# A kernel of two hybrid layers: 128x128 tiles turned by VectorE in 32x32 blocks in place of TensorE

## The chip, the cores and the metric

One core of one Trainium2 chip runs the whole kernel. The metric is the device time of one execution in microseconds; the kernel before takes 1930.4 us (median of 3 runs, 1929.9 to 1931.18).

## What is computed

Two layers (`DEPTH = 2`) over 256 tokens of width 2048. Each layer normalises x, multiplies it by one wide input weight, and gives the slices to four branches of width 512 (4 heads x 128): A, attention over keys that an indexer selects; B, chunked retention with rotary phase; C, a gated linear recurrence (HGRN2); M, attention into 256 memory tokens. Each branch is gated, projected, weighted by a sigmoid gate and summed; an output projection is added to x.

```python
h = rms_norm(x, norm_g)
u = h @ w_in
...
y_a = sparse_index_attention(head_rms_norm(heads(a_q), qk_g[0]), head_rms_norm(heads(a_k), qk_g[1]), ...)
y_b = retention(rope(heads(b_q), cos, sin), rope(heads(b_k), cos, sin) * HEAD_DIM ** -0.5, heads(b_v))
y_c = head_rms_norm(hgrn2(f, heads(c_i), heads(c_q)), hgrn_g)
y_m = memory_attention(head_rms_norm(heads(m_q), qk_g[2]), head_rms_norm(heads(m_k), qk_g[3]), heads(m_v))
for n, (y, z) in enumerate(((y_a, a_z), (y_b, b_z), (y_c, c_z), (y_m, m_z))):
    branch = y.reshape(B, S, W).astype(dt) * jax.nn.silu(z)
    merged = merged + jax.nn.sigmoid(gate_all[:, :, n]) * (branch @ w_branch[n])
return x + merged @ w_out
```

## The kernel before

All large products run on TensorE (PE). Both factors are split into a rounded part and a remainder (`hi`, `lo`), and each product is three matmuls, hi x hi, hi x lo and lo x hi (lines 234 to 236). The weights stream in as blocks of 512 rows by 512 columns (1024 KB, a few of 328 or 256 columns); `split_weights` (L201 to L210) cuts each block into two halves of 256 rows: ScalarE (ACT) casts a half to `whi` (L208), VectorE (DVE) subtracts to get `wlo` (L209). There are 674 such pieces, nearly all of 128x1024. A half feeds 12 matmuls of 128x512: 2 slices of 128 rows x 2 blocks of 128 tokens x 3 products. The pool holds `HL = 4` buffers each of `whi` and `wlo`, so the two engines can be at most four halves ahead of PE: the cast of half h waits until half h-4 is multiplied out, and every `wlo` stands in the one queue of DVE with all other work of DVE.

PE is in the order: memory keys and values for both layers (`mk`, `mv`), then per layer 16 projections (`u`), 16 pairs of gate projection and branch projection (`u`, `bw`), and 4 output projections (`wo`). The small work of the branches is written as generators. After each half `gemms` calls `stream.pump()` (L239), which lets the first task in the list that can move take one step up to its next `yield`; where a product needs a task's result, `finish` runs the task to its end. The order inside DVE, ACT, PE and GpSimd (POOL) is then set by the framework's scheduler, so that instructions of different halves can change places; SP's order is as written.

Wherever an operand has to be turned from tokens-by-channels to channels-by-tokens, `transposed` (L270) issues eight 128x128 transposes on PE against the identity `ident` into a PSUM tile (L275); attention turns its probabilities the same way (L377), the indexer its keys and queries (L404, L412). ACT then copies the PSUM tile to SBUF, often together with a scale or a sigmoid (L251, L311, L379, L406, L414, L467, L500, L508). One 128x1024 tile is eight such blocks. POOL does some elementwise products and sums (L330, L339, L390, L401, L461, L714) and the powers of `rsq` (L268).

Two places are followed below. In `head_norm` (L327) of the HGRN2 branch, with names that begin with `cn`: square (`cnsq`, ACT), sum (`cnss`, DVE), `cnv` (DVE), power (`cnr`, POOL), two products (`cny`), turn, split (`cnh` on ACT, `cnl` on DVE). In `attend` (L346) for the memory branch: `mlg` (logits, PE), `mmx` (row maximum, DVE), `mnm`, four exponentials (`mp`, ACT), `mrc` (reciprocal, DVE), turn (`mpT`), product with the values (`mov`, PE).

Of the kernel before, what the change touches and what calls it, by code (L numbers as in the profile page):

```python
# [91 lines left out]
class Stream:  # L92
    def __init__(self):
        self.loaded = self.cut = self.used = 0
        self.raw, self.parts, self.tasks = deque(), deque(), []
# [5 lines left out]

    def pump(self):
        for t in list(self.tasks):
            moved = t.step()
            if t.done:
                self.tasks.remove(t)
            if moved:
                return True
        return False

    def finish(self, t):
        while not t.done:
# [3 lines left out]
            elif not moved:  # L116
                ahead = self.tasks[:self.tasks.index(t)]
                assert any(u.step() for u in ahead)
# [31 lines left out]
def trunk(ctx: ExitStack, tc: tile.TileContext, x, xt, memt, ng, qkg, hg, lbl, win, wmem, wbr, wout,  # L150
# [120 lines left out]
    def transposed(src, name):  # L271
# [4 lines left out]
        return ps  # L276

# [12 lines left out]
    def normed_t(ps, rs, g, name):  # L290
# [16 lines left out]
        def turn():  # L307
            yield
            pt = transposed(qn, name + "pt")
            qt = G([128, 4, 256], name + "t")  # L310
            ac.activation(qt, pt, AF.Copy, scale=g)  # L311
            return qt
# [11 lines left out]
    def branch_t(y, name):  # L324
        return split(transposed(y, name + "pt"), gen, "g", name)

    def head_norm(ps, zs, g, name):  # L327
        v = ps.rearrange("p (a d) -> p a d", a=8)
        zg = G([128, 2, 512], name + "zg")
        po.tensor_tensor(zg, zs, g[:, None, :].to_broadcast([128, 2, W]), op=OP.mult)  # L330
# [8 lines left out]
        po.tensor_tensor(y, y1.rearrange("p (t h) d -> p t (h d)", t=2), zg, op=OP.mult)  # L339
        yield  # L340
        yield
        return branch_t(y, name)

    def attend(box, names, keys, name):
# [6 lines left out]
        for t in range(2):  # L351
# [22 lines left out]
            pp = PB(f"{name}pp{t}")[:, :4 * nk].rearrange("p (h s) -> p h s", h=4)  # L374
            for h in range(4):
                for b in range(nb):
                    te.transpose(pp[:, h, b * 128:b * 128 + 128], p[:, h, b * 128:b * 128 + 128], ident)  # L377
            pt = G([128, 4, nk], f"{name}pT{t}")
            ac.copy(pt, pp)  # L379
# [10 lines left out]
            po.tensor_tensor(y[:, t, :], on.rearrange("p h d -> p (h d)"), zs[:, t, :], op=OP.mult)  # L390
            yield
        yield
        yield
        yield
        return branch_t(y, name)

    def selection(qi0, qi1, name):
# [3 lines left out]
        po.tensor_copy(kk, qi1[:, :, None, 256:320].to_broadcast([128, 2, 2, 64]))  # L401
        ps = PB(name + "kp")
        for t in range(2):
            te.transpose(ps[:, t * 128:t * 128 + 128], kk[:, t].rearrange("p a d -> p (a d)"), ident)  # L404
        kit = G([128, 256], name + "kt")
        ac.copy(kit, ps[:, :256])  # L406
        yield
        ps = PB(name + "qp").rearrange("p (b t) -> p b t", b=4)
        for b in range(4):
            src = (qi0, qi1)[b // 2]  # L410
            for t in range(2):
                te.transpose(ps[:, b, t * 128:t * 128 + 128], src[:, t, (b % 2) * 128:(b % 2) * 128 + 128], ident)  # L412
        qit = G([128, 4, 256], name + "qt")
        ac.copy(qit, ps)  # L414
# [33 lines left out]
    def rope_t(ps, rs, name):  # L448
# [12 lines left out]
        po.tensor_tensor(a, a, b, op=OP.add)  # L461

        def turn():
            yield
            pt = transposed(a, name + "pt")
            o = G([128, 4, 256], name + "t")
            ac.copy(o, pt)  # L467
            return o
# [28 lines left out]
    def hgrn_scores(uf, uq, lb, olb, name):  # L497
        pf = transposed(uf, name + "fp")
        f = G([128, 4, 256], name + "f")
        ac.activation(f, pf, AF.Sigmoid)  # L500
# [5 lines left out]
        pq = transposed(uq, name + "qp")  # L506
        q0 = G([128, 4, 256], name + "q0")
        ac.copy(q0, pq)  # L508
# [134 lines left out]
    for l in range(L):  # L643
# [51 lines left out]
        def merged(acc, d):  # L695
            yield
            return split(transposed(acc, "mgp"), gen, "g", f"mg{d}")

        mg = []
        for d in range(4):  # L700
            acc = G([128, 2, 512], f"acc{d}")
            for i, n in enumerate(BR_ORDER):
# [9 lines left out]
                else:  # L712
                    ve.tensor_mul(gt, pb, gt)  # L713
                    (ve if i == 3 else po).tensor_tensor(acc, acc, gt, op=OP.add)  # L714
            mg.append(stream.add(merged(acc, d)))

        def turned(c, xc, nssq, l=l):
            yield
            r = split_scaled(transposed(xc, "xp"), ngs[:, l + 1, 4 * c:4 * c + 4], xtp, "xt", f"x1{c}")
# [67 lines left out]
```

## Time and profile before

| | |
|---|---|
| median of 3 runs | 1930.4 us |
| span of the profiled execution | 1928.6 us |
| PE busy | 1917.2 us, 99% |
| DVE busy | 1077.5 us, 56%, 1130 instructions |
| ACT busy | 884.1 us, 46% |
| POOL busy | 131.9 us, 7% |
| granted TensorE clock | 1.000 |

The span runs from the first to the last instruction of the profiled execution. Busy time of an engine counts stretches in which at least one of its instructions runs. A row of the groups gives line, engine, operation, tiles and shapes, count, then busy time and mean length of one in ns, then how long the engine stood idle before and for whom. A row of the waits names who waited for whom, with total, number of times and the longest. A row of the timeline gives start, length, engine, line, tiles and count.

### The profile page before, as it was taken

What the parts mean: (1) busy time and instruction counts of PE and PEld (TensorE: products, weight loads), DVE (VectorE), ACT (ScalarE), POOL (GpSimd) and SP (SyncE); (2) the same over time, 40 slices, a digit from 0 to 9 for tenths busy, and PEclk for the clock granted to TensorE, in tenths of its full rate; (3) what the DMA queues carried; (4) which work ended last, traced back from release to release, by engine and by line L of the source; (5) the groups of instructions that cost most, each with busy time, mean ns of one, the idle gap of its engine ahead of it and who ended that gap; (6) DMA issues with size and microseconds to landing.
All of it is one profiled execution on the core that took longest, in us unless ns stands there. A gap on an engine that the chain in (4) does not pass through costs nothing.

```text
span 1928.6 us, 22255 instructions
## 1 busy us (share of the span) xinstructions
PE 1917.2 (99%) x9068; PEld 1605.0 (83%) x9068; DVE 1077.5 (56%) x1130; ACT 884.1 (46%) x1011; POOL 131.9 (7%) x63
## 2 busy tenths in 40 slices
PE   8999999999999999999999999999999999999999
PEld 7888988888888888888888898888888888888887
DVE  6646685556555455545554658555555555555454
ACT  6543445445544444444445344544554444444442
POOL 0200100101010000001000010020101000000100
PEclk9999999999999999999999999999999999999999
DMA  9653555454455555555555354544445555555553
GB/s 370 231 202 110 187 173 176 165 185 165 162 196 195 190 186 194 196 195 190 183 191 194 107 191 171 178 172 175 174 158 193 195 196 185 189 196 194 197 195 111
DMA packets 53606, 357.36 MB, mean 185 GB/s; under 512 B 6272, under 2 KB 6656, under 8 KB 12544
## 3 DMA queue, kind: packets, MB, share of 16 engines
q1 hardware_dynamic: 53504, 355.94, 52.2%
q8 instruction: 71, 1.16, 0.2%
q14 instruction: 31, 0.25, 0.0%
HBM read 353.82 MB, written 2.10 MB: 185 GB/s over the span
## 4 chain that ended last, share of the span: by engine, by line
PE 99%; DMA 0%; ACT 0%; SPq 0%; issue 0%; DVE 0%; DVEq 0%; ACTq 0%
PE u L234 24%; PE u L235 23%; PE u L236 23%; PE wo L236 3%; PE wo L235 3%; PE bw L236 3%; PE bw L235 3%; PE bw L234 3%; PE wo L234 3%; PE cl L525 1%; PE mv L235 1%; PE mv L236 1%; PE mv L234 1%; PE mk L235 1%; PE mk L234 1%; PE mk L236 1%
## 5 line engine op out<-in xcount | busy, mean ns | idle before, releaser
L209 DVE TENSOR_TENSOR wlo<-raw,whi 128x1024 fp32r<-128x1024 f32 (+2 forms) x674 | 831.6, 1236 | 743.6 <-ACT whi L208 742.7
L208 ACT CAST whi<-raw 128x1024 fp32r<-128x1024 f32 (+2 forms) x674 | 696.3, 1034 | 975.8 <-PE u L236 764.5
L714 POOL TENSOR_TENSOR acc<-acc,gate 128x1024 f32<-128x1024 f32 x16 | 51.6, 3226 | 736.9 <-DVE gate L713 712.9
L234 PE MATMUL u<-whi,x11h 128*128 128x512 f32 (+2 forms) x256 | 99.3, 388 | 0.0
L234 PE MATMUL u<-whi,x10h 128*128 128x512 f32 (+2 forms) x256 | 98.8, 386 | 0.5 <-ACT qi L284 0.5
L234 PE MATMUL u<-whi,x00h 128*128 128x512 f32 (+2 forms) x256 | 98.7, 386 | 0.5 <-ACT qi L284 0.5
L234 PE MATMUL u<-whi,x01h 128*128 128x512 f32 (+2 forms) x256 | 99.3, 388 | 0.0
L235 PE MATMUL u<-wlo,x12h 128*128 128x512 f32 (+2 forms) x256 | 98.7, 386 | 0.0
L235 PE MATMUL u<-wlo,x02h 128*128 128x512 f32 (+2 forms) x256 | 98.7, 386 | 0.0
L235 PE MATMUL u<-wlo,x03h 128*128 128x512 f32 (+2 forms) x256 | 98.6, 385 | 0.0
L235 PE MATMUL u<-wlo,x13h 128*128 128x512 f32 (+2 forms) x256 | 98.6, 385 | 0.0
L236 PE MATMUL u<-whi,x13l 128*128 128x512 f32 (+2 forms) x256 | 98.6, 385 | 0.0
L236 PE MATMUL u<-whi,x03l 128*128 128x512 f32 (+2 forms) x256 | 98.6, 385 | 0.0
L234 PE MATMUL u<-whi,x02h 128*128 128x512 f32 (+2 forms) x256 | 98.6, 385 | 0.0
L234 PE MATMUL u<-whi,x12h 128*128 128x512 f32 (+2 forms) x256 | 98.6, 385 | 0.0
L234 PE MATMUL u<-whi,x03h 128*128 128x512 f32 (+2 forms) x256 | 98.5, 385 | 0.0
L234 PE MATMUL u<-whi,x13h 128*128 128x512 f32 (+2 forms) x256 | 98.5, 385 | 0.0
L236 PE MATMUL u<-whi,x02l 128*128 128x512 f32 (+2 forms) x256 | 98.4, 384 | 0.0
L236 PE MATMUL u<-whi,x12l 128*128 128x512 f32 (+2 forms) x256 | 98.4, 384 | 0.0
L236 PE MATMUL u<-whi,x10l 128*128 128x512 f32 (+2 forms) x256 | 98.4, 384 | 0.0
L235 PE MATMUL u<-wlo,x11h 128*128 128x512 f32 (+2 forms) x256 | 98.4, 384 | 0.0
L236 PE MATMUL u<-whi,x00l 128*128 128x512 f32 (+2 forms) x256 | 98.3, 384 | 0.0
(367 smaller groups left out, 3582.2 us busy)
## 6 DMA issues: line engine op xcount, KB each, us to landing
raw<-in_win SPq DMA_DIRECT2D x240, 1024.0 KB, 4.8
raw<-in_wbr SPq DMA_DIRECT2D x32, 1024.0 KB, 4.8
raw<-in_wout SPq DMA_DIRECT2D x32, 1024.0 KB, 4.8
raw<-in_wmem SPq DMA_DIRECT2D x15, 1024.0 KB, 8.2
raw<-in_win SPq DMA_DIRECT2D x8, 656.0 KB, 4.1
raw<-in_win SPq DMA_DIRECT2D x8, 512.0 KB, 3.4
xr<-in_xt SPq DMA_DIRECT2D x4, 512.0 KB, 9.8
xs<-in_x SPq DMA_DIRECT2D x4, 512.0 KB, 7.4
```

The source lines that it names most:

```text
L208: ac.copy(hi[:, a:b, :], r)
L209: ve.tensor_sub(lo[:, a:b, :], r, hi[:, a:b, :].bitcast(F32))
L234: te.matmul(ps[:, t, :n], ah[:, 2 * j + k, c], wh[:, k, :], start=first, stop=False)
L235: te.matmul(ps[:, t, :n], ah[:, 2 * j + k, c], wl[:, k, :], start=False, stop=False)
L236: te.matmul(ps[:, t, :n], al[:, 2 * j + k, c], wh[:, k, :], start=False, stop=last)
L525: te.matmul(ps[:, g * 64:g * 64 + 64].rearrange("p (b j) -> p b j", j=m), kd[:, g // 2, c], qd[:, g // 2, c].rearrange("p (b two j) -> p b ...
L714: (ve if i == 3 else po).tensor_tensor(acc, acc, gt, op=OP.add)
```

## The change

All turns but a few leave PE. A new helper `fold` turns a tile with VectorE's transpose, which works on 32x32 blocks: for each of the four groups of 32 source partitions and each of the four groups of 32 target partitions, one instruction turns all blocks of the tile that go from the one to the other (8 blocks, 32 partitions x 256 elements, for a whole tile; 4 or 2 blocks in smaller ones), and writes them straight into their target partitions: 16 instructions for a tile, from SBUF to SBUF. There is a `yield` after every four. The result needs no copy out of PSUM, so ACT's plain copies go and its scales and sigmoids work in place. Two kinds of turn stay on PE (`turned_at_once`): the last quarter of the merged branches (`d == 3`) and of the next layer's x (`c == 3`). In all 340 of 364 PE transposes go, and 752 DVE transposes come: 624 of 256 elements a partition, 96 of 128, 32 of 64.

All of POOL's elementwise products and sums, 36 in number, go to DVE (the four additions of B's rotary step, L461, the additions of L714, the products of L330, L339 and L390), and its copy of the indexer's keys (L401) to ACT. Some `yield`s are dropped, and `finish` and `scale_of` can now idle where no task moves.

```diff
@@ -268,12 +277,34 @@
         po.tensor_tensor(r, v, nhalf.to_broadcast([128, n]), op=OP.pow)
         return r
 
-    def transposed(src, name):
+    def fold(cuts, nb, name):
+        whole = G([128, nb, 128], name)
+        for i in range(4):
+            a = slice(32 * i, 32 * i + 32)
+            at = 0
+            for shape, src in cuts:
+                n = int(np.prod(shape))
+                for j in range(4):
+                    b = slice(32 * j, 32 * j + 32)
+                    part = whole[b, at:at + n, a]
+                    if len(shape) == 2:
+                        ve.transpose(part.rearrange("p (a b) c -> p a b c", a=shape[0]), src[a, :, :, b])
+                    else:
+                        ve.transpose(part, src[a, :, b])
+                at += n
+            yield
+        return whole
+
+    def turned_at_once(src, name):
         ps = PB(name).rearrange("p (h t) -> p h t", h=4)
         for h in range(4):
             for t in range(2):
                 te.transpose(ps[:, h, t * 128:t * 128 + 128], src[:, t, h * 128:h * 128 + 128], ident)
         return ps
+
+    def transposed(src, name):
+        u = yield from fold([((4, 2), src.rearrange("p t (h c) -> p h t c", h=4))], 8, name)
+        return u.rearrange("p (h t) c -> p h (t c)", h=4)
 
     def evac(ps, rs, name, n=512):
         u = G([128, 2, n], name)
@@ -306,10 +337,9 @@
 
         def turn():
             yield
-            pt = transposed(qn, name + "pt")
-            qt = G([128, 4, 256], name + "t")
-            ac.activation(qt, pt, AF.Copy, scale=g)
-            return qt
+            pt = yield from transposed(qn, name + "pt")
+            ac.activation(pt, pt, AF.Copy, scale=g)
+            return pt
         return turn()
 
     def gate_path(ps, rs, name):
@@ -322,12 +352,13 @@
         return zs
 
     def branch_t(y, name):
-        return split(transposed(y, name + "pt"), gen, "g", name)
+        u = yield from transposed(y, name + "pt")
+        return split(u, gen, "g", name)
 
     def head_norm(ps, zs, g, name):
         v = ps.rearrange("p (a d) -> p a d", a=8)
         zg = G([128, 2, 512], name + "zg")
-        po.tensor_tensor(zg, zs, g[:, None, :].to_broadcast([128, 2, W]), op=OP.mult)
+        ve.tensor_tensor(zg, zs, g[:, None, :].to_broadcast([128, 2, W]), op=OP.mult)
         sq = G([128, 8, 128], name + "sq")
         ac.activation(sq, v, AF.Square)
         ss = SM(8, name + "ss")
@@ -336,10 +367,9 @@
         y1 = G([128, 8, 128], name + "y1")
         ve.tensor_mul(y1, v, bc(r, HD))
         y = G([128, 2, 512], name + "y")
-        po.tensor_tensor(y, y1.rearrange("p (t h) d -> p t (h d)", t=2), zg, op=OP.mult)
+        ve.tensor_tensor(y, y1.rearrange("p (t h) d -> p t (h d)", t=2), zg, op=OP.mult)
         yield
-        yield
-        return branch_t(y, name)
+        return (yield from branch_t(y, name))
 
     def attend(box, names, keys, name):
         qt = yield from wait_for(box, names[0])
@@ -371,12 +401,8 @@
             rc = SM(4, f"{name}rc{t}")
             ve.reciprocal(rc, sm)
             yield
-            pp = PB(f"{name}pp{t}")[:, :4 * nk].rearrange("p (h s) -> p h s", h=4)
-            for h in range(4):
-                for b in range(nb):
-                    te.transpose(pp[:, h, b * 128:b * 128 + 128], p[:, h, b * 128:b * 128 + 128], ident)
-            pt = G([128, 4, nk], f"{name}pT{t}")
-            ac.copy(pt, pp)
+            pt = yield from fold([((4 * nb,), p.rearrange("p h (b s) -> p (h b) s", b=nb))], 4 * nb, f"{name}pT{t}")
+            pt = pt.rearrange("p (h b) s -> p h (b s)", h=4)
             v = yield from wait_for(box, names[2])
             yield
             ov = PB(f"{name}ov{t}")[:, :512].rearrange("p (h d) -> p h d", h=4)
@@ -387,31 +413,22 @@
             on = G([128, 4, 128], f"{name}on{t}")
             ve.tensor_mul(on, ov, bc(rc, HD))
             zs = yield from wait_for(box, names[3])
-            po.tensor_tensor(y[:, t, :], on.rearrange("p h d -> p (h d)"), zs[:, t, :], op=OP.mult)
+            ve.tensor_tensor(y[:, t, :], on.rearrange("p h d -> p (h d)"), zs[:, t, :], op=OP.mult)
             yield
         yield
-        yield
-        yield
-        return branch_t(y, name)
+        return (yield from branch_t(y, name))
 
     def selection(qi0, qi1, name):
         wv = SM(16, name + "w").rearrange("p (t h) -> p t h", t=2)
         ve.tensor_scalar(wv, qi1[:, :, 320:328], NIH ** -0.5, None, op0=OP.mult)
         kk = G([128, 2, 2, 64], name + "kk")
-        po.tensor_copy(kk, qi1[:, :, None, 256:320].to_broadcast([128, 2, 2, 64]))
-        ps = PB(name + "kp")
-        for t in range(2):
-            te.transpose(ps[:, t * 128:t * 128 + 128], kk[:, t].rearrange("p a d -> p (a d)"), ident)
-        kit = G([128, 256], name + "kt")
-        ac.copy(kit, ps[:, :256])
+        ac.copy(kk, qi1[:, :, None, 256:320].to_broadcast([128, 2, 2, 64]))
         yield
-        ps = PB(name + "qp").rearrange("p (b t) -> p b t", b=4)
-        for b in range(4):
-            src = (qi0, qi1)[b // 2]
-            for t in range(2):
-                te.transpose(ps[:, b, t * 128:t * 128 + 128], src[:, t, (b % 2) * 128:(b % 2) * 128 + 128], ident)
-        qit = G([128, 4, 256], name + "qt")
-        ac.copy(qit, ps)
+        kit = yield from fold([((2,), kk.rearrange("p t a d -> p t (a d)"))], 2, name + "kt")
+        kit = kit.rearrange("p t s -> p (t s)")
+        qit = yield from fold([((2, 2), u[:, :, :256].rearrange("p t (b c) -> p b t c", b=2)) for u in (qi0, qi1)],
+                              8, name + "qt")
+        qit = qit.rearrange("p (b t) s -> p b (t s)", b=4)
         masks = []
         for t in range(2):
             nk = 128 * (t + 1)
@@ -458,14 +475,11 @@
             for lo, hi in ((0, 64), (64, 0)):
                 ve.scalar_tensor_tensor(bv[:, :, lo:lo + 64], pv[:, :, hi:hi + 64], rs[:, t:t + 1],
                                         st[:, :, lo:lo + 64], op0=OP.mult, op1=OP.mult)
-        po.tensor_tensor(a, a, b, op=OP.add)
+        ve.tensor_tensor(a, a, b, op=OP.add)
 
         def turn():
             yield
-            pt = transposed(a, name + "pt")
-            o = G([128, 4, 256], name + "t")
-            ac.copy(o, pt)
-            return o
+            return (yield from transposed(a, name + "pt"))
         return turn()
 
     def mix_values(blocks, v, name):
@@ -495,17 +509,14 @@
         return (lambda h: s0[:, h, 0:128]), (lambda h: s0[:, h, 128:256]), (lambda h: s1[:, h, :])
 
     def hgrn_scores(uf, uq, lb, olb, name):
-        pf = transposed(uf, name + "fp")
-        f = G([128, 4, 256], name + "f")
-        ac.activation(f, pf, AF.Sigmoid)
+        f = yield from transposed(uf, name + "f")
+        ac.activation(f, f, AF.Sigmoid)
         for h in range(4):
             ve.tensor_scalar(f[:, h, :], f[:, h, :], olb[:, h:h + 1], lb[:, h:h + 1], op0=OP.mult, op1=OP.add)
         yield
         kd = G([128, 4, 256], name + "k")
         ve.tensor_scalar(kd, f, -1.0, 1.0, op0=OP.mult, op1=OP.add)
-        pq = transposed(uq, name + "qp")
-        q0 = G([128, 4, 256], name + "q0")
-        ac.copy(q0, pq)
+        q0 = yield from transposed(uq, name + "q0")
         qd = G([128, 4, 256], name + "q")
         ve.tensor_mul(qd, q0, f)
         yield
@@ -693,8 +704,12 @@
         box[key("mz")] = gate_path(proj(O_MZ), rs, "mz")
 
         def merged(acc, d):
-            yield
-            return split(transposed(acc, "mgp"), gen, "g", f"mg{d}")
+            if d == 3:
+                yield
+                u = turned_at_once(acc, "mgp")
+            else:
+                u = yield from transposed(acc, "mgp")
+            return split(u, gen, "g", f"mg{d}")
 
         mg = []
         for d in range(4):
@@ -711,19 +726,24 @@
                     ve.tensor_mul(acc, pb, gt)
                 else:
                     ve.tensor_mul(gt, pb, gt)
-                    (ve if i == 3 else po).tensor_tensor(acc, acc, gt, op=OP.add)
+                    ve.tensor_tensor(acc, acc, gt, op=OP.add)
             mg.append(stream.add(merged(acc, d)))
 
         def turned(c, xc, nssq, l=l):
-            yield
-            r = split_scaled(transposed(xc, "xp"), ngs[:, l + 1, 4 * c:4 * c + 4], xtp, "xt", f"x1{c}")
+            if c == 3:
+                yield
+                u = turned_at_once(xc, "xp")
+            else:
+                u = yield from transposed(xc, "xp")
+            r = split_scaled(u, ngs[:, l + 1, 4 * c:4 * c + 4], xtp, "xt", f"x1{c}")
             for t in range(2):
                 sq = G([128, 512], "xsq")
                 ac.activation(sq, xc[:, t, :], AF.Square, accum_out=nssq[:, t * 4 + c:t * 4 + c + 1])
             return r
 
-        def scale_of(nssq):
-            yield
+        def scale_of(nssq, ready):
+            while not all(t.done for t in ready):
+                yield BLOCKED
             return rms(nssq, 1)
 
         if l + 1 < L:
```

The first place is DVE's queue at the end of the HGRN2 branch of the first layer. Names beginning with `cn` are that branch's norm, `ixkk`, `ixkt`, `ixqt`, `qi` and `ixw` belong to the indexer; `wlo` is the remainder of a weight half, the tile that PE waits for. Before:

```order
L334 TENSOR_REDUCE cnss<-cnsq 128x8
L209 TENSOR_TENSOR wlo<-raw,whi 128x656
L266 TENSOR_SCALAR cnv<-cnss 128x8
L209 TENSOR_TENSOR wlo<-raw,whi 128x656 x2
L337 TENSOR_TENSOR cny_1614<-co,cnr 128x1024
L209 TENSOR_TENSOR wlo<-raw,whi 128x656 x2
L209 TENSOR_TENSOR wlo<-raw,whi 128x1024 x2
L252 TENSOR_TENSOR cnl<-cnpt,cnh 128x1024
L209 TENSOR_TENSOR wlo<-raw,whi 128x1024 x2
L399 TENSOR_SCALAR ixw<-qi_1879 128x16
```

The same place now:

```order
L218 TENSOR_TENSOR wlo<-raw,whi 128x1024
L365 TENSOR_REDUCE cnss<-cnsq 128x8
L275 TENSOR_SCALAR cnv<-cnss 128x8
L368 TENSOR_TENSOR cny_1693<-co,cnr 128x1024
L370 TENSOR_TENSOR cny<-cny_1693,cnzg 128x1024
L291 STREAM_TRANSPOSE cnpt<-cny 32x8x32 x16
L261 TENSOR_TENSOR cnl<-cnpt,cnh 128x1024
L218 TENSOR_TENSOR wlo<-raw,whi 128x1024
L423 TENSOR_SCALAR ixw<-qi_1914 128x16
L293 STREAM_TRANSPOSE ixkt<-ixkk 32x2x32 x14
L218 TENSOR_TENSOR wlo<-raw,whi 128x1024
L293 STREAM_TRANSPOSE ixkt<-ixkk 32x2x32 x2
```

Before, a `wlo` stood between any two steps of the chain; now the whole chain, with its 16 transposes and the second product that was POOL's, stands between two of them, and the indexer's 48 transposes follow. On PE the last product of `co`, from which the chain starts, stands in front of the half whose `wlo` comes four later than the last one done.

The second place is DVE's queue in the memory attention of the first layer, first half of the tokens. Before:

```order
L209 TENSOR_TENSOR wlo<-raw,whi 128x1024 x5
L363 TENSOR_REDUCE mmx_3560<-mlg_3539 128x4
L365 TENSOR_SCALAR mnm_3562<-mmx_3560 128x4
L372 RECIPROCAL mrc_3570<-msm_3565 128x4
L209 TENSOR_TENSOR wlo<-raw,whi 128x1024 x4
L388 TENSOR_TENSOR mon_3626<-mov_3617,mrc_3570 128x512
```

The same place now:

```order
L218 TENSOR_TENSOR wlo<-raw,whi 128x1024
L393 TENSOR_REDUCE mmx_3838<-mlg_3817 128x4
L395 TENSOR_SCALAR mnm_3840<-mmx_3838 128x4
L402 RECIPROCAL mrc_3848<-msm_3843 128x4
L293 STREAM_TRANSPOSE mpT_3868<-mp_3842 32x8x32 x14
L218 TENSOR_TENSOR wlo<-raw,whi 128x1024
L293 STREAM_TRANSPOSE mpT_3868<-mp_3842 32x8x32 x2
L218 TENSOR_TENSOR wlo<-raw,whi 128x1024 x4
```

The wait for the four exponentials, which ends at `mrc`, stood alone between two `wlo` before; now 14 of the 16 transposes stand behind it ahead of the next `wlo`.

More of the change, by code (lines that the diff above doesn't have):

```diff
@@ L93, in __init__ @@
     def __init__(self):
-        self.loaded = self.cut = self.used = 0
+        self.loaded = self.cut = self.used = self.ticks = self.idle = 0
         self.raw, self.parts, self.tasks = deque(), deque(), []
@@ L100, in add, with rest @@
         return t
+    def rest(self, n):
+        until = self.ticks + n
+        while self.ticks < until:
+            yield BLOCKED
     def pump(self):
+        self.ticks += 1
         for t in list(self.tasks):
@@ L117, in finish @@
                 ahead = self.tasks[:self.tasks.index(t)]
-                assert any(u.step() for u in ahead)
+                if not any(u.step() for u in ahead):
+                    self.ticks += 1
+                    self.idle += 1
+                    assert self.idle < 1000
                 self.tasks = [u for u in self.tasks if not u.done]
@@ L723, in turned @@
             return r
-        def scale_of(nssq):
-            yield
+        def scale_of(nssq, ready):
+            while not all(t.done for t in ready):
+                yield BLOCKED
             return rms(nssq, 1)
@@ L741, in trunk @@
         if l + 1 < L:
-            xh, rs = nx, stream.add(scale_of(nssq))
+            xh, rs = nx, stream.add(scale_of(nssq, list(nx)))
 def _cols(w, chunks):
```

## The prediction

> **What bounds the kernel now.** I read the page's head and its chain first.
>
> ```profile
> span 1928.6 us, 22255 instructions
> ...
> PE 1917.2 (99%) x9068; PEld 1605.0 (83%) x9068; DVE 1077.5 (56%) x1130; ACT 884.1 (46%) x1011; POOL 131.9 (7%) x63
> ...
> PE 99%; DMA 0%; ACT 0%; SPq 0%; issue 0%; DVE 0%; DVEq 0%; ACTq 0%
> ```
>
> PE is busy from end to end, and 99% of the chain that ended last is PE. So what PE no longer has to do is saved, as long as PE is never made to wait. The waits say how near that is.
>
> ```profile
> ACT whi L208 <- PE u L236: 764.5, 462, 5.3
> DVE wlo L209 <- ACT whi L208: 742.7, 547, 3.8
> ...
> PE mk L234 <- ACT memh L562: 4.9, 1, 4.9
> ...
> PE mv L235 <- DVE wlo L209: 0.8, 1, 0.8
> ```
>
> PE waits once for 4.9 us, at the start, and for a `wlo` once, 0.8. ACT waits for PE to free a weight buffer, and DVE for ACT: the pair that prepares the weights is always as far ahead as the four buffers let it. How much room that leaves is read from PE's timeline and from the groups of the two steps.
>
> ```profile
> 900.43 0.39 PE L235 MATMUL u<-wlo,x01h 128*128 128x512 f32 x1
> ...
> 903.15 0.39 PE L235 MATMUL u<-wlo,x01h 128*128 128x512 f32 x1
> ```
> ```profile
> L208 ACT CAST whi<-raw 128x1024 fp32r<-128x1024 f32 x638 | 672.0, 1054 | 925.6 <-PE u L236 720.2 <-PE wo L236 85.0 <-PE bw L236 65.2
> ```
> ```profile
> L209 DVE TENSOR_TENSOR wlo<-raw,whi 128x1024 fp32r<-128x1024 f32 x638 | 802.0, 1259 | 719.7 <-ACT whi L208 718.9
> ```
>
> The two matmuls are 12 apart in PE's order, one half of a weight block: a half takes 2.72 us, a matmul 0.227. DVE owes one `wlo` of 1.26 us in each 2.72, which leaves it 1.46 us a half on average. A burst may be longer. Count from the end of half h-4: the cast ends at about 1.1, `wlo` h at 2.4. PE starts half h+1 at 4 x 2.72 = 10.9 and reads its `wlo` from the second matmul, at 11.1. Between two `wlo`, DVE can then do 11.1 - 2.4 - 1.3 = **7.4 us** of other work at most. What is longer stops PE, and right behind it only 1.46 us a half are free, until DVE has caught up.
>
> **What goes.** One burst of eight PE transposes in the timeline:
>
> ```profile
> 600.13 0.39 PE L236 MATMUL u<-whi,x01l 128*128 128x512 f32 x1
> 600.36 1.03 PE L275 MATMUL mgp<-csb,acc 128*128 128x128 f32 x8
> 601.15 0.48 PE L234 MATMUL u<-whi,x01h 128*128 128x512 f32 x1
> 601.46 0.40 PE L235 MATMUL u<-wlo,x01h 128*128 128x512 f32 x1
> ```
>
> Without it the matmul at 601.46 would start at 600.36 + 0.23 = 600.59. Eight transposes cost PE 0.87 us, one 0.109. 340 of them go: 340 x 0.109 = **37.2 us**, all on the path. ACT's copies of the turned tiles out of PSUM also go; ACT is 46% busy and waits for PE, so they count for nothing. SP's queue and the loads stay as they are.
>
> **What comes.** 752 transposes on DVE, an operation that the trace does not have. The nearest rows are those of other DVE instructions with 256, 128 or 64 elements in a partition:
>
> ```profile
> L441 DVE MAX8 ixm<-ixsc 128x8 f32<-128x256 f32 x16 | 6.8, 426 | 0.4
> L435 DVE SCALAR_TENSOR_TENSOR ixsc<-ixrl,ixw,ixsc 128x256 f32<-128x256 f32 x14 | 6.7, 482 | 0.3
> L442 DVE MATCH_REPLACE8 ixsc<-ixm,ixsc 128x256 f32<-128x256 f32 x16 | 6.5, 409 | 0.0
> ...
> L441 DVE MAX8 ixm<-ixsc 128x8 f32<-128x128 f32 x16 | 4.7, 295 | 0.6
> ...
> L563 DVE TENSOR_TENSOR meml<-memr,memh 128x256 fp32r<-128x256 f32 x2 | 0.8, 418 | 0.0
> ...
> L444 DVE TENSOR_SCALAR ixmk<-ixsc 128x256 f32<-128x256 f32 x2 | 0.6, 294 | 0.1
> ...
> L539 DVE TENSOR_TENSOR cT<-cT 128x64 f32<-128x64 f32 x2 | 0.5, 226 | 0.1
> ```
> ```profile
> 339.88 1.22 DVE L209 TENSOR_TENSOR wlo<-raw,whi 128x1024 fp32r<-128x1024 f32 x1 [0.35 <-ACT whi L208]
> ...
> 344.21 2.36 DVE L209 TENSOR_TENSOR wlo<-raw,whi 128x1024 fp32r<-128x1024 f32 x2 [0.76 <-ACT whi L208]
> ```
>
> Three operations of 256 elements take 409 to 426 ns. I take **0.42 us**, and 0.29 and 0.23 for 128 and 64 elements. The upper bound is L435, 0.48. Below there are two: two `wlo` without a wait between them take 2.36 us where one takes 1.22, so an instruction can overlap its neighbour by 0.08, which makes 0.34; and L444 does 256 elements in 0.29. I choose 0.42, without overlap, as the middle of the rows that are most alike: one result per element read, none faster.
>
> On the overlap the Trainium skill speaks against this change: its page "VectorE: DVE Perf Modes", section "Two Vector instructions with no wait between them", has it that an instruction whose output begins in another group of 32 partitions than the last output starts only when all earlier ones have ended. `fold` changes that group with every instruction, so by that rule there is no overlap; no instruction of this trace tests it. The same page, section "The three transpose paths", gives 311 ns for a transpose of 128 bf16 elements, against the 295 and 275 that such rows take here; by it, 256 elements would take some 0.44, an estimate, and the sum below would be some 10 us worse.
>
> Moved from POOL to DVE are 36 products and sums, 28 of 1024 and 8 of 512 elements:
>
> ```profile
> L714 DVE TENSOR_TENSOR acc<-acc,gate 128x1024 f32<-128x1024 f32 x8 | 9.7, 1218 | 0.0
> ...
> L388 DVE TENSOR_TENSOR aon<-aov,arc 128x512 f32<-128x512 f32 x4 | 2.8, 688 | 0.3 <-PE aov L385 0.3
> ```
>
> 28 x 1.22 + 8 x 0.69 = 40 us, and the transposes 624 x 0.42 + 96 x 0.29 + 32 x 0.23 = 297. DVE grows from 1077 to about 1415 us, 73% of the span. On average that fits, and where the merged branches are turned (one tile in 40 halves) the burst of 16 x 0.42 = 6.7 us is below 7.4. What costs time are the places where bursts meet.
>
> *End of the HGRN2 branch.* The whole chain stands between two `wlo`.
>
> ```profile
> L334 DVE TENSOR_REDUCE cnss<-cnsq 128x8 f32<-128x1024 f32 x2 | 2.4, 1220 | 3.1 <-ACT cnsq L332 3.1
> L337 DVE TENSOR_TENSOR cny<-co,cnr 128x1024 f32<-128x1024 f32 x2 | 2.4, 1216 | 0.0
> ```
> ```profile
> L332 ACT ACTIVATE cnsq<-co 128x1024 f32<-128x1024 f32 x2 | 2.1, 1028 | 2.8 <-PE co L480 2.8
> L251 ACT CAST cnh<-cnpt 128x1024 fp32r<-128x1024 f32 x2 | 2.0, 1016 | 2.3 <-PE cnpt L275 2.3
> ```
> ```profile
> L268 POOL TENSOR_TENSOR cnr<-cnv,nhalf 128x8 f32<-128x8 f32 x2 | 4.5, 2244 | 2.3 <-DVE cnv L266 2.3
> ```
>
> From the end of `co` on PE: 1.03 square, 1.22 sum, about 0.2 `cnv`, 2.24 power, 1.22 + 1.22 products, 16 x 0.42 = 6.72 transposes, 1.02 cast, about 1.22 remainder, 1.26 `wlo`: 17.3 us. PE has four halves in hand, 11.1 us: it stops for 6.2. Then the indexer's transposes follow, again one `wlo` behind each group: 0.2 (`ixw`) + 14 x 0.23 + 1.26 = 4.7 against 2.72; 2 x 0.23 + 13 x 0.29 + 1.26 = 5.5; 12 x 0.29 + 1.26 = 4.7; 7 x 0.29 + 1.26 = 3.3: 2.0, 2.8, 2.0 and 0.6 more. Together 13.6 a layer, 27 in both.
>
> *Memory attention.* Its chain runs in the trace of before already:
>
> ```profile
> 469.21 1.73 PE mlg L356 x8
> ```
> ```profile
> 470.97 1.22 DVE L363 TENSOR_REDUCE mmx<-mlg 128x4 f32<-128x1024 f32 x1 [0.32 <-PE mlg L356]
> ...
> 475.76 0.18 DVE L372 RECIPROCAL mrc<-msm 128x4 f32<-128x4 f32 x1 [3.36 <-ACT mp L369]
> ```
>
> From the end of `mlg` (470.94) to that of `mrc` (475.94) it takes 5.0 us, 3.4 of them DVE waiting for ACT. With 14 x 0.42 = 5.9 and a `wlo` of 1.26 behind it that is 12.2 against 11.1 or, where `mlg` stands a matmul into a half, 10.9: about 1.2 us, four times, 5 us.
>
> *Others.* In branch A the keys' transposes follow the queries' (16, then 4, 7 and 4 between single `wlo`): 7.0 (with 0.3 of the mask) and the top-k steps just before, 1.2 together, are 0.5 to 0.8 over 7.4, then 0.2, 1.5 and 0.2 (7 x 0.42 + 1.26 = 4.2 against 2.72): 2.5 a layer. The same sum gives 1.7 for B's queries and keys, 1 for `cf` and `cq`, and about 1 for the attention over selected keys. Together 6 a layer, 12 in both.
>
> The sum: 27 + 5 + 12 = **44 us of new waits against 37 saved**: 1928.6 + 7 = 1935.6 for the span. The median of the runs is 1.8 above this span, so **1938 us**. By the same places 0.48 gives 71 us of waits (1965 in the metric); 0.34 gives 17 at the HGRN2 branch and next to nothing elsewhere (1911); 0.29 gives about 10 (1903). The sum crosses zero near 0.40.
>
> **The rivals.** *Overlap.* Transposes start before their neighbours end, or are as quick as L444: 0.29 to 0.34. DVE catches up, PE loses its 340 transposes and stops only at the HGRN2 branch: 1903 to 1911, faster. For it: independent DVE work in this trace does overlap. Against it: L441 and L442, single instructions of the same size, are above 0.40, and the output changes its partitions each time. It decides below 0.40.
>
> *Slow blocks.* Turning 4-byte elements costs a second pass. From 128 to 256 elements L441 grows by 0.13, so 256 more would make about 0.42 + 0.26 = 0.68. 16 x 0.68 = 10.9, 3.5 over what fits, 39 times, makes 137 us, and the indexer's 128 smaller ones, at most 0.26 each longer, 33: with the 44 some 214, 2107 us. Nothing in the trace speaks for it.
>
> *Nothing saved on PE.* If the turns ran in time that PE loses anyway (its matmuls, 0.227 apart, would then be paced by something else), 44 us would come and none go: 1974. Against it: the next two matmuls are late by the whole 0.87.
>
> **How the numbers follow.** About 0.2% (4 us) is what a measurement of this kernel can tell from no change. Forecast, 0.40 to 0.48 and waits as summed (1926 to 1965): 0.50, of which 0.04 faster, 0.09 the same, 0.37 slower, since 0.42 lies near the zero. Overlap: 0.33, faster. Slow blocks, with prices above 0.48: 0.12. Nothing saved: 0.05. So faster 0.37, same 0.09, slower 0.54. The range goes from the fastest price, 1903, to 1975, a little beyond 0.48, with the slow blocks left out.
>
> **What would show it.** The transposes' mean length and their distance in DVE's timeline; waits of PE for DVE `wlo`, none today beyond 0.8 us, with a stop of 6 us behind each `co` and three or four of 2 to 3 behind it; PE's busy time down by about 37; DVE at 73%. If the distance is 0.42 and PE does not stop at `co`, the buffer reasoning is wrong. If the distance is 0.34 or less and PE still stops for 40 us, the waits are not those of bursts. A clock below 1.000 or a DMA wait for `raw` would be something that I have not counted.

## The result, and the profile after

The changed kernel takes **1958.33 us** (median of 4 runs, 1956.75 to 1959.67) against 1930.79 for the kernel before (median of 4): a ratio of 1.0142, 95% interval 1.0128 to 1.0156. It is slower by 1.4%; the runs of either kernel lie within 3 us. The profiled execution has a span of 1955.2 us at a clock of 0.993.

The head of the page and its chain that ended last:

```profile
span 1955.2 us, 22231 instructions
...
PE 1902.7 (97%) x8728; PEld 1576.5 (81%) x8728; DVE 1381.6 (71%) x1918; ACT 863.6 (44%) x991; POOL 31.9 (2%) x25
...
PE 80%; DVE 15%; issue 2%; ACT 1%; DMA 0%; POOL 0%; SPq 0%; POOLq 0%; DVEq 0%; ACTq 0%
```

DVE is only 71% busy and yet 15% of the chain, where it was 0%: it is late in places, not on average. PE's waits say for what:

```profile
PE u L244 <- DVE wlo L218: 30.0, 28, 2.9
PE bw L244 <- DVE wlo L218: 5.2, 2, 2.7
PE mk L243 <- ACT memh L573: 4.9, 1, 4.9
PE u L243 <- ACT qi L315: 3.7, 2, 1.8
PE u L243 <- ACT whi L217: 2.9, 2, 1.5
```

Thirty stops of projections and branch products for a `wlo` stand there, where only the one of 0.8 us at the memory values stood. The groups give the price of the new operation, by size, and of `wlo`:

```profile
L218 DVE TENSOR_TENSOR wlo<-raw,whi 128x1024 fp32r<-128x1024 f32 x638 | 772.3, 1222 | 450.0 <-ACT whi L217 447.0
L291 DVE STREAM_TRANSPOSE mgp<-acc 32x256 f32<-32x256 f32 x96 | 41.9, 436 | 1.6
...
L291 DVE STREAM_TRANSPOSE ixqt<-qi 32x128 f32<-32x128 f32 x64 | 19.4, 303 | 1.0
...
L293 DVE STREAM_TRANSPOSE ixkt<-ixkk 32x64 f32<-32x64 f32 x32 | 7.5, 236 | 0.4
```

A transpose of 256 elements takes 0.436 us. In DVE's timeline twelve in a row take 5.38, 0.448 each, so none starts before the one ahead has ended:

```profile
614.92 5.38 DVE L291 STREAM_TRANSPOSE mgp<-acc 32x256 f32<-32x256 f32 x12
```

The end of the HGRN2 branch in the first layer, first DVE's timeline, then PE's:

```profile
227.08 1.23 DVE L218 TENSOR_TENSOR wlo<-raw,whi 128x1024 fp32r<-128x1024 f32 x1 [1.21 <-ACT whi L217]
228.84 1.22 DVE L365 TENSOR_REDUCE cnss<-cnsq 128x8 f32<-128x1024 f32 x1 [0.54 <-ACT cnsq L363]
...
232.01 1.23 DVE L368 TENSOR_TENSOR cny<-co,cnr 128x1024 f32<-128x1024 f32 x1 [1.75 <-POOL cnr L277]
...
234.53 7.18 DVE L291 STREAM_TRANSPOSE cnpt<-cny 32x256 f32<-32x256 f32 x16
242.83 1.23 DVE L261 TENSOR_TENSOR cnl<-cnpt,cnh 128x1024 fp32r<-128x1024 f32 x1 [1.11 <-ACT cnh L260]
243.97 1.22 DVE L218 TENSOR_TENSOR wlo<-raw,whi 128x1024 fp32r<-128x1024 f32 x1
```
```profile
227.36 0.39 PE L494 MATMUL co<-ci,cA 128*128 128x128 f32 x2
229.59 0.51 PE L243 MATMUL u<-whi,x00h 128*128 128x512 f32 x1 [1.84 <-ACT qi L315]
...
230.33 0.63 PE L245 MATMUL u<-whi,x00l 128*128 128x512 f32 x1
230.75 0.63 PE L243 MATMUL u<-whi,x00h 128*128 128x512 f32 x1
...
243.79 0.50 PE L243 MATMUL u<-whi,x02h 128*128 128x512 f32 x1 [1.41 <-ACT whi L217]
245.24 0.50 PE L244 MATMUL u<-wlo,x02h 128*128 128x512 f32 x1 [0.95 <-DVE wlo L218]
...
249.96 0.51 PE L244 MATMUL u<-wlo,x02h 128*128 128x512 f32 x1 [1.70 <-DVE wlo L218]
...
255.84 0.50 PE L244 MATMUL u<-wlo,x03h 128*128 128x512 f32 x1 [2.82 <-DVE wlo L218]
```

DVE does no `wlo` between 228.31 and 243.97. From the end of `co` (227.75) to that of the next `wlo` (245.19) it is 17.4 us. PE stops at 227.75, 242.4, 244.3, 248.3 and 253.0. Between 229.95 and 233.4 its matmuls are 0.43 apart in place of 0.227: after the stop the clock granted is half.

**Where the time went.** I took, for each matmul, the distance to the next start, and set it against the median of the same form in the trace of before. Without the 340 transposes PE has 36.7 us less to do. Distances that exceed it by more than 0.1 us, the stops and the one slower matmul behind each, add up to an excess of 64.2 us against 10.7 before, 53.5 more. Seven stretches at half clock, of 3.41 us each, cost 9.9. 1928.6 - 36.7 + 53.5 + 9.9 = 1955.3, the span.

### The profile page after: what moved, and what is told of

It reads as the page before. It is cut to its first block, busy times and chain, and to the rows that moved or that the text cites. A ratio compares the mean times of both kernels' runs of the same rounds, so it can differ in the third digit from the quotient of the medians.

```text
span 1955.2 us, 22231 instructions
## 1 busy us (share of the span) xinstructions
PE 1902.7 (97%) x8728; PEld 1576.5 (81%) x8728; DVE 1381.6 (71%) x1918; ACT 863.6 (44%) x991; POOL 31.9 (2%) x25
## 4 chain that ended last, share of the span: by engine, by line
PE 80%; DVE 15%; issue 2%; ACT 1%; DMA 0%; POOL 0%; SPq 0%; POOLq 0%; DVEq 0%; ACTq 0%
PE u L244 18%; PE u L245 18%; PE u L243 18%; DVE wlo L218 4%; PE bw L244 3%; PE bw L245 3%; PE bw L243 3%; PE wo L244 3%; PE wo L245 3%; PE wo L243 3%; PE cl L536 1%; DVE mpT L293 1%; PE mv L244 1%; DVE ixqt L291 1%; PE mv L245 1%
## 5 line engine op out<-in xcount | busy, mean ns | idle before, releaser
L218 DVE TENSOR_TENSOR wlo<-raw,whi 128x1024 fp32r<-128x1024 f32 (+2 forms) x674 | 799.4, 1198 | 475.1 <-ACT whi L217 472.0
L244 PE MATMUL u<-wlo,x10h 128*128 128x512 f32 (+2 forms) x256 | 99.5, 389 | 0.8 <-DVE wlo L218 0.8
L244 PE MATMUL u<-wlo,x01h 128*128 128x512 f32 (+2 forms) x256 | 98.8, 386 | 1.5 <-DVE wlo L218 1.4
L244 PE MATMUL u<-wlo,x00h 128*128 128x512 f32 (+2 forms) x256 | 99.4, 388 | 0.3 <-DVE wlo L218 0.3
## 6 DMA issues: line engine op xcount, KB each, us to landing
xr<-in_xt SPq DMA_DIRECT2D x4, 512.0 KB, 10.2
```

Source lines behind the costliest of these rows:

```text
L218: ve.tensor_sub(lo[:, a:b, :], r, hi[:, a:b, :].bitcast(F32))
L244: te.matmul(ps[:, t, :n], ah[:, 2 * j + k, c], wl[:, k, :], start=False, stop=False)
```

## The experiments

The theory on which they were made is the prediction's: PE really is relieved of 37 us, and loses more to stops because bursts of transposes on DVE hold up a `wlo` for longer than four buffers last. Three rivals are tried: the turns saved nothing on PE; the moved products and sums overload DVE; the order that the scheduler gave DVE is to blame.

**Six buffers in place of four.** In the changed kernel (label e1) and, as a control, in the kernel before (e2):

```diff
-GEN, HL, RAW = 18, 4, 4
+GEN, HL, RAW = 17, 6, 3
```

> The changed kernel with six buffers of whi and wlo in place of four (to make room, raw has three in place of four and the general pool 17 in place of 18). If PE stops because bursts of DVE work between two wlo exceed what four halves cover (7.4 us), the room grows by two halves, 2 x 2.72, to 12.8 us: only the chain at the end of the HGRN2 branch (some 17 us) still exceeds it. PE's waits for wlo fall from 35 us to under 15, and the time to 1900 to 1920 us. If the waits come from something else (the order on PE, ACT standing behind a transpose, the throttle by itself), it stays at 1945 to 1960.

> The kernel before with the same buffers (six, three, 17): the control of the run above. PE never waits there, so both theories expect no change: 1930 us, within 3.

Measured: 1914.17 us, ratio 0.9916 (0.9901 to 0.993) for the changed kernel; 1930.47, ratio 1.0 (0.999 to 1.001) for the one before. The waits of the first:

```profile
PE u L244 <- DVE wlo L218: 9.9, 9, 2.6
```

With two more halves in hand 21 of the 30 stops go, and the time falls by 44 us; the kernel before, which had no such stops, gains nothing. At B's norm the same 13 transposes and a sum, and two more transposes (three with six buffers), stand between two `wlo`, and PE no longer stops there: that is depth alone. In other places the scheduler changed DVE's order too (in the memory attention a `wlo` now stands between the maximum and `mrc`), and what depth and order gain there is not separated. Without most of its stops the change is a gain.

**POOL keeps its products and sums** (the changed kernel with the 36 operations back on `po`, for example):

```diff
-        ve.tensor_tensor(a, a, b, op=OP.add)
+        po.tensor_tensor(a, a, b, op=OP.add)
```

> The changed kernel, but the 36 products and sums stay on POOL as before; DVE turns the tiles. If the bursts of transposes are the cost, DVE is 40 us less busy, but mostly where it had room; the chain at the end of a branch loses 1.2 us of DVE and gains POOL's 2.4 to 2.9: 1948 to 1965 us. Rival: the work moved from POOL is what overloads DVE; then most of the 28 us go: 1925 to 1938 us.

Measured: 1965.57, ratio 1.0181 (1.0166 to 1.0196), 7 us slower than the changed kernel and just above the range expected.

```profile
PE u L244 <- DVE wlo L218: 34.7, 30, 3.2
```
```profile
L218 DVE TENSOR_TENSOR wlo<-raw,whi 128x1024 fp32r<-128x1024 f32 x638 | 799.1, 1265 | 466.4 <-ACT whi L217 463.3
```

The moved work is not what costs: with it back on POOL the time is longer. But the expectation had DVE 40 us less busy, and it is not (1380.1 us, 1381.6 in the changed kernel). The mean `wlo` is back at 1.265 us, 0.043 longer, and the second product at the end of the HGRN2 branch takes 2.38 us on POOL and 1.23 on DVE. Which of the two makes the 7 us was not tried apart.

**Calm places only**: the kernel before, with `fold` only in the merged branches (`d < 3`) and the next layer's x (`c < 3`), 72 turns.

```diff
-            return split(transposed(acc, "mgp"), gen, "g", f"mg{d}")
+            if d == 3:
+                yield
+                u = transposed(acc, "mgp")
+            else:
+                u = yield from folded(acc, "mgp")
+            return split(u, gen, "g", f"mg{d}")
...
```

> The kernel before, with only the tiles turned by DVE that fall where DVE has room: three of four quarters of the merged branches and of the next layer's x, 72 of the 340 transposes. Each is one burst of 16 x 0.436 = 7.0 us, under 7.4, with no other burst near: PE saves 72 x 0.109 = 7.8 us and does not stop: 1922 to 1925 us. If a burst by itself stops PE, nine of them at 1 to 2 us take the gain back: 1930 us or more.

Measured: 1922.6, ratio 0.9959 (0.9944 to 0.9974). The saving expected is 72 x 0.109 = 7.8 us, the measured one 7.9. PE's waits are those of before. A burst of 16 between `wlo` that are on time costs nothing.

**The same partitions**: each turned block is written to the partitions that it was read from. The blocks are turned but not moved, so this kernel leaves a part of the turn out and does not give the program's result. The 752 instructions keep their sizes, and the group of output partitions changes only four times a tile.

```diff
-                    part = whole[b, at:at + n, a]
+                    part = whole[a, at:at + n, b]
```

> The changed kernel, but each transpose writes into the partitions that it reads (the blocks are turned and not moved, so what follows computes on wrong data); 16 instructions a tile as before, and now the output's partitions change only with every fourth. If an instruction whose output starts elsewhere than the last one's waits for it to end, three of four now overlap by 0.08: distance 0.36 us, mean near 0.37, and the time falls to 1925 to 1940 us. If the turning itself takes 0.434, nothing changes: 1955 to 1960 us.

Measured: 1915.4, ratio 0.992 (0.9905 to 0.9935), lower than expected. A group and twelve in a row:

```profile
L291 DVE STREAM_TRANSPOSE mgp<-acc 32x256 f32<-32x256 f32 x96 | 34.0, 405 | 0.5
```
```profile
594.71 4.28 DVE L291 STREAM_TRANSPOSE mgp<-acc 32x256 f32<-32x256 f32 x12
```

Now they are 0.357 apart, less than the 0.405 that each takes. Start by start in the trace, over all whole tiles, the mean distance is 0.33 to 0.37 where the output stays in the group of 32 partitions of the one before, and 0.40 to 0.41, without overlap, where the group changes after every fourth. In the changed kernel it is 0.44 to 0.45 at each of the 16, also at the blocks that stay in their own partitions; so it is the change of group from one output to the next that costs, and not the moving. The overlap of neighbours exists, and writing to other partitions than the instruction ahead takes it away. That is what the Trainium skill says ("VectorE: DVE Perf Modes", section "Two Vector instructions with no wait between them"); the trace agrees, with 0.357 against 0.448. With 0.09 us less in each on average, the stops for a `wlo` fall from 35.2 us to 8.4 (with 2.7 under `bw`) and the granted clock is 1.000. So the price of one transpose decides the sign, as the prediction had it: by its own sums 0.34 gives 1911 and 0.42 gives 1938.

**A quarter of the transposes**: four instructions over all 128 partitions for a tile, which turns each block in its own partitions and leaves the moving out; this kernel does not give the program's result either.

```diff
-                for j in range(4):
-                    b = slice(32 * j, 32 * j + 32)
-                    part = whole[b, at:at + n, a]
...
+                part = whole[:, at:at + n, a]
```

> The changed kernel, but a tile is turned by 4 instructions over all 128 partitions, each turning its blocks in place within their partitions (three quarters of the work is left out, and what follows computes on wrong data). The code, the tasks and the tiles stay. If the amount of transposes between two wlo is the cost, a burst takes 1.7 us, PE stops only for the rest of the chain at the HGRN2 branch: 1897 to 1908 us. If the changed order of the chains or of PE costs by itself, 1920 us or more remain.

Measured: 1897.97, ratio 0.983 (0.9815 to 0.9844).

```profile
PE 1880.3 (99%) x8728; PEld 1570.7 (83%) x8728; DVE 1144.5 (60%) x1354; ACT 863.8 (46%) x991; POOL 30.8 (2%) x25
```
```profile
PE u L243 <- ACT qi L313: 3.7, 2, 1.8
PE u L244 <- DVE wlo L218: 1.5, 2, 0.8
```

PE's busy time is 36.9 us under that of before, and 33.1 of it are gained (1931.05 for the kernel before beside these runs). "Nothing saved on PE" is ruled out.

**DVE in the order as written**, in the changed kernel, in it with six buffers, and in the kernel before:

```diff
-        with tc.manual_schedule(engines={mybir.EngineType.SP}):
+        with tc.manual_schedule(engines={mybir.EngineType.SP, mybir.EngineType.DVE}):
```

> The changed kernel with DVE's instructions in the order in which the code writes them (the scheduler no longer reorders DVE): the same 752 transposes, but four of them, 1.74 us, between two wlo in place of up to 16. With 1.74 + 1.22 = 2.96 a half against PE's 2.72, a tile puts DVE 1 us behind, inside the 7.4 us that the buffers cover. If the bunching is what stops PE, its waits for wlo fall from 35 us to under 10 and the time to 1895 to 1910 us. If the amount of DVE work (71% busy) or ACT's place in the chains is the cost, the time stays at 1940 to 1960 us.

> The run above with six buffers of whi and wlo besides (raw three, general pool 17). If what is left there are chains that hold one wlo for longer than 7.4 us, the room of 12.8 us takes most of them: 1893 to 1900 us, near the floor of 1930.5 - 34 = 1896. If DVE written in this order loses in other ways (an instruction that stands behind another engine), six buffers change little.

> The kernel before with DVE's instructions in the order in which the code writes them: the control of the run in which the changed kernel got that order and stayed at 1961 us with other waits than before. If the written order by itself costs (single chains of sum, power and products that hold a wlo back, 4.6 to 5.4 us each at the ends of the branches), the kernel before loses some 15 to 30 us by it too: 1945 to 1962 us. If those waits come from the transposes in any order, it stays at 1930 to 1935 us.

Measured: 1960.92 (ratio 1.0157, 1.014 to 1.0173), 1973.28 (1.0218, 1.0202 to 1.0233) and 1984.68 (1.028, 1.0264 to 1.0295). The first two expectations failed: the changed kernel came out at about the time that was expected if the amount of DVE's work or ACT's place in the chains is the cost. The third held in direction, and the loss is larger than expected. Waits of the changed kernel in this order:

```profile
PE u L244 <- DVE wlo L218: 29.3, 15, 5.5
...
PE cl L536 <- DVE cT L550: 4.9, 6, 1.2
```

There are half as many stops for a `wlo`, the longest twice as long, and others come, behind the steps of the chains. The third run tells why that does not decide against the theory: the written order costs the kernel before 54 us by itself. Within it the change gains 24 us, 1984.7 to 1960.9. So what the transposes cost depends on the order they are put into, but this order is no remedy. Six buffers make it 12 us slower still, with stops of up to 6.5 us for a `wlo` and 16 us of waits for `whi` and `gate`; why, stays open. Deeper buffers are shown to help in the scheduler's order only.

**Turns at the end of the HGRN2 branch back on PE**, with six buffers: `cn` and the indexer (e10), and with them those of the attention's probabilities (e11).

```diff
-        u = yield from transposed(y, name + "pt")
+        if name == "cn":
+            yield
+            u = turned_at_once(y, name + "pt")
+        else:
+            u = yield from transposed(y, name + "pt")
...
-            pt = yield from fold([((4 * nb,), p.rearrange("p h (b s) -> p (h b) s", b=nb))], 4 * nb, f"{name}pT{t}")
...
+                    te.transpose(pp[:, h, b * 128:b * 128 + 128], p[:, h, b * 128:b * 128 + 128], ident)
...
```

The first part is in both, the second in e11 alone; the indexer's turns and the buffers, in both, are not shown.

> The changed kernel with six buffers (raw three, general pool 17), and with the turns at the end of the HGRN2 branch and of the indexer on PE again, as before: 36 of the 340. PE saves 304 x 0.109 = 33 us; of the 18 us of waits that six buffers left, those at the branch end (12 us and 4 us of half clock) go: 1898 to 1904 us. If the chain stops PE without its transposes too (power, products), it stays at 1908 to 1914 us.

> The run above with the turns of both attentions' probabilities on PE too, 92 of the 340: PE saves 248 x 0.109 = 27 us. If six buffers cover the attention's bursts anyway, this only gives 6 us back: 1904 to 1909 us. If those bursts still stop PE, it is as fast as the run above or faster.

Measured: 1930.96, ratio 1.0 (0.9991 to 1.001), and 1941.5, ratio 1.0055 (1.004 to 1.007). Both missed. PE's waits in e10:

```profile
PE cnpt L302 <- DVE cny L374: 7.0, 1, 7.0
PE cnpt L302 <- issue: 6.9, 1, 6.9
PE u L243 <- ACT gate L732: 5.0, 2, 2.5
```

No wait for a `wlo` in the layers is left, but PE itself now stands for 7 us a layer at the turn `cnpt`: in PE's order it follows `co` directly, and the chain of square, sum, power and products runs in between. Behind it comes half clock, 10.2 us in each layer. In e11 the 56 further turns cost PE 6.1 us, and its waits for `gate` grow from 5.0 to 7.5.

**And those at the branch's start too**: the kernel before with six buffers and `fold` everywhere but at `cf`, `cq`, `cn`, the indexer and the last quarters, 272 turns; POOL keeps its work.

```diff
     def branch_t(y, name):
-        return split(transposed(y, name + "pt"), gen, "g", name)
+        if name == "cn":
+            return split(transposed(y, name + "pt"), gen, "g", name)
+        u = yield from folded(y, name + "pt")
+        return split(u, gen, "g", name)
...
```

> The changed kernel with six buffers for `wlo` and the small work back on GpSimd; on TensorE stay the turns of `cf` and `cq` (ahead of the chain of HGRN2), of `cn` (behind it), of the indexer and of the last quarters, 272 of the 640 are left to VectorE. In the order of TensorE the turn `cnpt` now stands seven half-generations (each 12 products) behind the last `co`, where it stood directly behind it in the kernel with the branch's end on TensorE and six buffers. If it was that missing distance which cost the 7.0 and 6.9 us there, they are gone: 272 x 0.109 us = 29.7 us off the kernel before, 1901, and some waits behind the bursts of 16 transposes, 1901 to 1912. If instead TensorE has to stand at the end of this branch wherever other turns are on VectorE (rival), `cnpt` still shows stops of several us in each layer and the time is 1915 to 1932.

Measured: 1912.67, ratio 0.9906 (0.9889 to 0.9922), 0.7 above the 1901 to 1912 expected.

```profile
PE u L234 <- ACT gate L727: 5.9, 2, 3.0
...
PE u L234 <- DVE akn L327: 2.6, 2, 1.3
PE mov L405 <- DVE mpT L291: 1.9, 2, 1.1
```

No stop at `cnpt` is left: 85 matmuls, 12.4 us, stand between the last `co` and `cnpt`, as in the kernel before, and none did in e10. The run differs from e10 in more than that, but POOL's product makes the chain in between longer and not shorter; so it was the place of the turn in PE's order that made PE stand there. (The expectation says 272 of 640; counted in 128x128 turns as the prediction does, it is 272 of 364.) What stays is ACT, which stands behind the exponentials of the attention while PE waits for a gate. The time lies in the same interval as six buffers alone: fewer stops, but 68 more turns on PE, 7.4 us. Either version beats the kernel before by 0.8 to 0.9%, and the changed kernel by 2.2 to 2.3%.

## Why the prediction was right

The direction and the mechanism were right: PE saves its 37 us, no transpose overlaps the next, and bursts longer than the buffers last stop PE for more than was saved. The size was not: some 7 us of loss were forecast, 27.5 came. The direction was also a narrow call, 0.54 for slower, since the forecast is a small difference of two large terms and crosses zero near 0.40. The two terms that it left out, 5.9 and 9.9 us, both happened to add to the loss; that the direction came out so clearly is partly luck.

**The saving.** 37.2 us were forecast, 36.7 are found between the matmuls of the changed kernel and 36.9 in the run with a quarter of the transposes. PE's busy time in the changed kernel fell by only 14.5, so the sign "PE busy down by about 37" was a bad one: busy time also counts matmuls at half clock, and a longer one behind each stop (0.50 in place of 0.39).

**The price.** 0.42 was chosen, 0.436 is the mean and 0.448 the distance, inside the forecast's own 0.40 to 0.48; the prediction's other estimate, 0.44, was the nearer one. On its own scale, 44 us of waits at 0.42 and 71 at 0.48, the difference is worth some 7 to 13 us, an estimate. That there is no overlap was right, and the runs show the cause. The smaller ones cost 0.303 and 0.236, against 0.29 and 0.23. "Slow blocks" did not come.

**The waits.** They were summed at 44 us, and are 53 and 10 of half clock. By place, both layers, less what the same places cost before:

| place | forecast | stops | half clock |
|---|---|---|---|
| end of HGRN2, indexer | 27 | 20.3 | 5.8 |
| memory attention | 5 | 10.7 | 4.1 |
| A, B, `cf`/`cq`, selected keys | 12 | 16.3 | 0 |
| B's norm and M's queries | 0 | 5.9 | 0 |

The first row holds almost to the microsecond, 26 for 27, though it does not look as forecast. The chain from `co` to the `wlo` behind it takes 17.4 us against 17.3. But no stop of 6.2 us follows: PE first stands for `qi`, which ACT does behind `cnsq`; then runs at half clock and so uses up its halves more slowly; then waits for a `whi`, because ACT has stood in `cnh` for 12 us behind the transposes with the casts of weights behind it; and only then, 0.95 us, for the `wlo`. The sum is what counts, and it is set by DVE: from the last `co` to the matmul that reads this `wlo`, half clock included, PE loses 6.6 us in the first layer and 6.7 in the second, 0.8 of which it lost there before, for the 6.2 forecast.

```profile
ACT cnh L260 <- DVE cnpt L291: 24.5, 2, 12.3
```

**What was mis-sized** is the step on the memory attention, 1.2 us each where 2.7 and 1.8 stand in the first layer. Timelines of that place, PE's `mlg`, then DVE:

```profile
496.20 1.89 PE L386 MATMUL mlg<-mk0pt,mqpt 128*128 128x256 f32 x8
```
```profile
497.89 1.21 DVE L218 TENSOR_TENSOR wlo<-raw,whi 128x1024 fp32r<-128x1024 f32 x1
499.02 1.22 DVE L393 TENSOR_REDUCE mmx<-mlg 128x4 f32<-128x1024 f32 x1
...
504.06 0.18 DVE L402 RECIPROCAL mrc<-msm 128x4 f32<-128x4 f32 x1 [3.62 <-ACT mp L399]
504.16 6.24 DVE L293 STREAM_TRANSPOSE mpT<-mp 32x256 f32<-32x256 f32 x14
510.43 1.23 DVE L218 TENSOR_TENSOR wlo<-raw,whi 128x1024 fp32r<-128x1024 f32 x1
```

The row maximum starts 0.9 us after `mlg` has ended, where it started at once before: DVE was still catching up with `wlo` after the turn of M's queries. The transposes take 6.24 in place of 5.9, and the wait for ACT 3.6 in place of 3.4. 13.6 us from `mlg` to the `wlo`, less 10.9 in hand, is 2.7, the stop measured.

**What was left out.** Two things. Bursts that fit one by one into 7.4 us were put at nothing: the norm of B has 13 transposes, a sum of 1.22 and two more transposes between two `wlo`, 5.83 + 1.22 + 0.89 = 7.9, and the turn of M's queries follows before DVE has caught up. And half clock was not priced, 10 us; the prediction named a clock below 1.000 only as something that it had not counted. Against that DVE's `wlo` came 0.04 us cheaper than assumed. The span is 19.6 us longer than the 1935.6 forecast: 9.2 from stops (-6.7, +5.7, +4.3 and +5.9 by the rows of the table), 9.9 from half clock and 0.5 from the saving.

## What to carry to other kernels

Here, work moved from the engine that bounds to one that is 56% busy was free only in pieces shorter than the buffers between the two last; sum the pieces that stand between two deliveries, whole chains and neighbouring bursts included, before counting the saving. If they don't fit, deepen the buffers first, which here turned 1.4% lost into 0.8% gained. Keeping the turns around a latency chain on the old engine gained nothing beyond that, and where the turn followed the chain's start directly in that engine's order it cost the whole gain. An average load shows neither.

## What the runs showed of the hardware

*Half clock after a stop of under 2 us.* PE's timeline at two stops of the same length, in the two layers:

```profile
538.11 0.51 PE L244 MATMUL u<-wlo,x02h 128*128 128x512 f32 x1 [1.82 <-DVE wlo L218]
538.45 0.40 PE L245 MATMUL u<-whi,x02l 128*128 128x512 f32 x1
538.69 0.40 PE L243 MATMUL u<-whi,x02h 128*128 128x512 f32 x1
```
```profile
1464.89 0.50 PE L244 MATMUL u<-wlo,x12h 128*128 128x512 f32 x1 [1.83 <-DVE wlo L218]
...
1465.79 0.63 PE L244 MATMUL u<-wlo,x12h 128*128 128x512 f32 x1
1466.22 0.63 PE L245 MATMUL u<-whi,x12l 128*128 128x512 f32 x1
```

Behind the first the matmuls go on 0.24 apart, behind the second 0.43. The seven stretches of half clock inside the run last 3.41 us each and begin at multiples of 3.413 us from one another (229.95, 257.26 and 513.26 are 8 and 75 of them apart). If the run is cut into cells of this length, the seven cells just ahead of the half clock hold 1.83 to 2.85 us of idle PE, and no other cell of the layers more than 1.70; the stop at 538 falls on a border, 0.86 in one cell and 0.96 in the next. In other runs the line is less sharp (in e1 a cell with 1.84 stayed at full clock, in e3 one with 1.71 did not). So a stop of about half a cell can cost up to 1.7 us more, half of a stretch, by where it falls. The Trainium skill has the grid and the halving ("TensorE: Matmul & The Clock Gate", Part 1), but asks for an idle window of some 3.4 us; here half of one sufficed.

*POOL's work slows DVE.* The mean `wlo` of 1024 elements takes 1.26 us or more in every kernel in which POOL does its products and sums (1.30 in e9), and 1.22 in every one in which it does not: over 638 of them some 27 us of DVE, two thirds of the 40 that the moved work costs. The mean hides how. In the kernel before, 612 of the 638 take 1.22 us (one 1.25) as all of them do in the changed kernel; the other 26 take 1.4 to 3.3, and each of these overlaps an instruction of POOL, 24 of them one of its products and sums. So a `wlo` is held up now and then, for 2 us at most, and not slowed throughout. That is most of why giving the work back to POOL left DVE as busy as it was.
